# Two-layer decoder on one core: the second tile's residual put before weight splits, and the last queries transposed earlier

## The chip, the cores and the metric

The kernel runs on one core of one Trainium2 chip. The metric is the device time of one execution in microseconds (us), lower is better. The core has TensorE (PE, with PEld for its weight loads), VectorE (DVE), ScalarE (ACT), GpSimd (POOL) and SyncE (SP, which issues the DMAs).

## The reference

A sequence of 256 tokens of width 1024 goes through two layers, each `x <- x + RMSNorm_post(mixer(RMSNorm_pre(x)))`. All arithmetic is float32. Layer 0 is a chunked gated linear attention. Layer 1 is a sparse attention with three branches: compressed blocks, selected blocks and a window. For these sizes the selected and window branches see all keys up to the causal limit. Cut to what matters here:

```
def reference(x, positions, pre_norm, post_norm, ...):
    for i in range(2):
        h = rms_norm(x, pre_norm[i])
        y = gla_mixer(h, ...) if i == 0 else nsa_mixer(h, positions, ...)
        x = x + rms_norm(y, post_norm[i])
    return x

def nsa_mixer(h, positions, w_in, b_gate, ..., w_out):
    q, kc, vc, ks, vs, kw, vw, gl, z = split(h @ w_in)
    q, kc, ks, kw = rope(each, positions)        # q is also scaled by 1/8
    ...
    o = sum over branches of sigmoid(gl + b_gate) * attention(q, branch)
    return (o * silu(z)) @ w_out
```

## The kernel before, in words

**Tiles.** The 256 tokens are two tiles (t = 0, 1) of 128 rows. A float32 product is made from three fp32r matmuls: each operand is split into a rounded part `hi` and a rest `lo`, and hi*hi, hi*lo and lo*hi are summed (`mm3`, lines 211 to 213). Weights come in chunks of up to 512 columns (`Chunk`): a DMA brings two rows of 128 (`raw`, four buffers), ACT writes `hi` (line 190) and DVE or POOL writes `lo` (line 196). Which engine writes `lo` is listed per chunk in `LOS`; for the chunk of the selected keys, `ch_ks`, it is DVE for the rows k = 0 to 3 and POOL for 4 to 7. `hi` and `lo` have eight buffers each.

**The order of the work.** The order on each engine is made when the program is built: a scheduler plays the program through in its own simulated time and takes, on each engine, the earliest traced instruction that is ready in that time. `after(a, b)` forces a to be issued after b. `chain` lines up projections on PE in the order written; instructions outside it, such as most transposes, fall where the scheduler finds room. `paced` is a hint that ties weight splits to the progress of another projection. Buffers of one tag are shared by all tiles of that tag.

**The layer boundary.** For each tile, `out_proj` (line 340) makes layer 0's output in two halves n = 0, 1 in PSUM. `residual` (line 263) follows: ACT squares each half (line 269, with a sum), DVE adds the sums (lines 271, 274), POOL takes the power (line 275), DVE multiplies each half by the norm's row (line 276) and adds the result to X (line 281). Its two tiles `yg` share the tag `xg` (two buffers) with the tile of the same name in `pre_T`. `pre_T` (line 298) transposes X on PE (line 302), scales it (DVE, line 307) and splits it into `hT` (ACT line 310, DVE line 311). `rms` (line 318) squares X for the next norm. After both tiles, `ch_kc` (compressed keys and values) and `ch_ks` (selected keys and values) are split; `ch_ks.split_unit(ks_after)` issues the two `hi` of its first unit after the last line 310 of tile 0, and `ch_ks.split()` does the other three units with no such tie. Then `kc_part(0)`, `ks_part(0)`, `kc_part(1)` and `ks_part(1)` project: each is 24 matmuls of 512 columns into one of two `acc` banks. `kc_part` also ropes its keys (lines 821 to 827) and transposes the result (line 853, 32 small matmuls); for t = 0 it transposes the position vectors (line 846). Loads of the next weights reuse layer 0's memory, the row of its post norm too, which line 276 reads last.

**The attention stage.** `q_steps(p, t)` projects and ropes 8 of the 16 heads for a tile; `q_T(p, t)` transposes them on PE (line 982) into a bank of tag `t` (two banks) and copies them in halves by ACT and DVE (lines 987, 988) into a tile of tag `qS` (six buffers). A `Unit(g, t)` is one of four groups of heads in one tile: `scores` (line 1020, four heads), softmax (DVE 1025, ACT 1027), weighing by POOL (line 1061), `values` with transposes of the weights (line 1091, 1111, banks of tag `t`), copies (1095, 1097), and matmuls (1105, 1129). `finish` gates the result and splits it into `ofT` of its tile; the four tiles of `ofT` have the tag `qS` too. `z_steps(p)` is a projection in 8 steps (k) of 12 chained matmuls. `out_steps(t)` is the last projection; its weights `ch_o` are split under a pace by the steps of `z_steps(1)`. Near the end the program reads, in order: `q_T(1, 0)`, the splits of `ch_z[1]`, `q_steps(1, 1)`, `unit(2, 0)`, `q_T(1, 1)`, `z_steps(1)`, `unit(3, 0)`, `out_steps(0)`, the four units of tile 1, `out_steps(1)`.

Of the kernel before, what the change touches and what calls it, by code (L numbers as in the profile page):

```python
# [10 lines left out]
F32R = mybir.dt.float32r  # L11
I32 = mybir.dt.int32
AF = mybir.ActivationFunctionType
# [3 lines left out]
P = 128  # L17
# [70 lines left out]
def hybrid_kernel(ctx: ExitStack, tc: tile.TileContext, x, positions, pre_norm, post_norm,  # L88
# [9 lines left out]
    def nm(s):  # L98
        _n[0] += 1
        return f"{s}_{_n[0]}"  # L100

    def bank(tag="t"):
        return ps.tile([P, 512], F32, tag=tag, name=nm(tag), bufs=BANKS[tag])
# [4 lines left out]
    def after(ins, prev):  # L108

        if prev is not None:  # L110
            tc.add_manual_dep(ins.ins, prev.ins.name, mybir.DependencyInfo(
                mybir.DependencyClass.NoSync, mybir.DependencyReason.DATA), reason="issue order")
        return ins
# [103 lines left out]
    def chain(first, final):  # L217

        after(first, last[0])
        last[0] = final  # L220
# [34 lines left out]
    def rstd_of(ss, n, m, by=1.0):  # L255
# [4 lines left out]
        nc.gpsimd.tensor_tensor(r[:, :m], v[:, :m], half[:, :m], op=ALU.pow)  # L260
        return r

    def residual(t, o, gb):

        ss = base.tile([P, 8], F32, tag="ss", name=nm("ss"), bufs=4)
        yg = [base.tile([P, H], F32, tag="xg", name=nm("yg"), bufs=2) for _ in range(2)]

        def done(n):
            nc.scalar.activation(yg[n], o[n], AF.Square, accum_out=ss[:, n:n + 1])  # L269
            if n == 0:  # L270
                nc.vector.tensor_scalar(ss[:, 2:3], ss[:, 0:1], D * EPS, None, op0=ALU.add)
            else:

                nc.vector.tensor_add(ss[:, 4:5], ss[:, 1:2], ss[:, 2:3])
                nc.gpsimd.tensor_tensor(ss[:, 3:4], ss[:, 4:5], half[:, :1], op=ALU.pow)
            nc.vector.scalar_tensor_tensor(yg[n], o[n], float(D ** 0.5), gb[:, n * H:(n + 1) * H], op0=ALU.mult,  # L276
                                           op1=ALU.mult)
            if n == 1:
                for m in range(2):
                    xx = X[:, t, m * H:(m + 1) * H]  # L280
                    nc.vector.scalar_tensor_tensor(xx, yg[m], ss[:, 3:4], xx, op0=ALU.mult, op1=ALU.add)
        return done
# [12 lines left out]
        nc.scalar.activation(hi, bv, AF.Copy)  # L295
        nc.vector.tensor_sub(lo, bv, f(hi))

    def pre_T(t, c, layer, hT, tag, prev=None):

        b = bank(tag)  # L300
        for k in range(4):
            m = nc.tensor.transpose(b[:, k * P:(k + 1) * P], X[:, t, (c * 4 + k) * P:(c * 4 + k + 1) * P], ident)
            if layer == t == 0:
                chain(m, m)
        xg = base.tile([P, 4, P], F32, tag="xg", name=nm("xg"), bufs=2)
        g = gT[:, layer * KT + c * 4:layer * KT + c * 4 + 4]
        nc.vector.tensor_tensor(xg, b.rearrange("p (k n) -> p k n", k=4), g.unsqueeze(2).to_broadcast([P, 4, P]),
                                op=ALU.mult)
        hi, lo = (a[:, c * 4:c * 4 + 4, t * P:(t + 1) * P] for a in hT)
        m = after(nc.scalar.activation(hi, xg, AF.Copy), prev)  # L310
        nc.vector.tensor_sub(lo, xg, f(hi))  # L311
        return m

    onesr = base.tile([P, P], F32R, tag="onesr", name="onesr")
    nc.gpsimd.tensor_copy(onesr, ones)
# [458 lines left out]
    for t in range(NT):  # L774
        out_proj(t, ch_o, oT, gpost)
        for c in range(2):
            last_hi = pre_T(t, c, 1, hT, "t")
        if t == 0:
            ks_after = last_hi
        rs1.append(rms(t)[0])  # L780
        for tab in (CSt, SNt):
            nc.vector.tensor_scalar(tab[:, t], tab[:, t], rs1[t], None, op0=ALU.mult)
# [3 lines left out]
    lp = ctx.enter_context(tc.tile_pool(name="l2", bufs=1))  # L786
    ch_kc.split()
    ch_ks = Chunk(w_in, N_KS, 512).load()
    ch_ks.split_unit(ks_after)
    ch_ks.split()  # L790
    vs_sb = lp.tile([P, NT, 256], F32, tag="vs", name="vs_sb")
    vw_sb = lp.tile([P, NT, 256], F32, tag="vw", name="vw_sb")
# [23 lines left out]
    def rope(o, nh, t, twice):  # L816

        ov = o.rearrange("p (h a d) -> p h a d", a=2, d=HD)
        t1 = lp.tile([P, 8, 2, HD], F32, tag="rt1", name=nm("rt1"), bufs=2)
        t2 = lp.tile([P, 8, 2, HD], F32, tag="rt2", name=nm("rt2"))  # L820
        nc.vector.tensor_mul(t1[:, :nh], ov, CSt[:, t].unsqueeze(1).to_broadcast([P, nh, 2, HD]))
        for a in range(2):
            nc.vector.tensor_mul(t2[:, :nh, a, :], ov[:, :, 1 - a, :],
                                 SNt[:, t, a, :].unsqueeze(1).to_broadcast([P, nh, HD]))
        a, b = (y[:, :nh].rearrange("p h a d -> p h (a d)") for y in (t1, t2))
        if not twice:
            nc.gpsimd.tensor_add(a, a, b)
            return a
        r = cp.tile([P, nh, 2, DH], F32, tag="dup", name=nm("dup"), bufs=2)
        nc.gpsimd.tensor_add(r, *(y.unsqueeze(2).to_broadcast([P, nh, 2, DH]) for y in (a, b)))  # L830
        return r
# [5 lines left out]
            nc.tensor.transpose(b[:, g * P:(g + 1) * P], r[:, g].rearrange("p e d -> p (e d)"), ident)  # L837
        return b

    def kc_part(t):  # L840
        o = proj(ch_kc, hT, t)
        rv = cp.tile([P, GROUPS, DH], F32, tag="rv", name=nm("rv"), bufs=2)
        nc.scalar.activation(rv, o[:, 256:512].rearrange("p (g d) -> p g d", d=DH), AF.Copy, scale=rs1[t])
        if t == 0:
            b = bank("o")
            nc.tensor.transpose(b[:, :32], vecs, ident[:32, :32])
            nc.vector.tensor_copy(vT, b[:, :32])

        b = bank()
        for kv, r in enumerate((rope(o[:, :256], 4, t, False), rv)):  # L850
            for g in range(GROUPS):
                for two in range(2):
                    nc.tensor.matmul(b[two * 64:(two + 1) * 64, kv * 256 + g * 64:kv * 256 + (g + 1) * 64], r[:, g],
                                     ident[:, two::2], start=(kv == g == 0), stop=True, skip_group_check=True)
        bv = b.rearrange("p (k g c r) -> p k g c r", k=2, g=GROUPS, r=8)
        for half in range(2):

            c0 = 1 if half and not t else 0
            n = 8 - c0
            at = t * 8 + c0 - half  # L860
            for kv in range(2):
                v = vT[:, kv * 16 + half * 8:kv * 16 + half * 8 + 8]
                nc.vector.tensor_tensor(flat[:, half, kv, :, :, at:at + n].rearrange("p r g c -> p g c r"),
                                        bv[:, kv, :, c0:], v.unsqueeze(1).unsqueeze(1)
                                        .to_broadcast([P, GROUPS, n, 8]), op=ALU.add)
# [6 lines left out]
    def ks_part(t):  # L872
        o = proj(ch_ks, hT, t)
        nc.scalar.activation(vs_sb[:, t, :], o[:, 256:512], AF.Copy, scale=rs1[t])
        k_T(o, t, (1 - t) * P)

    kc_part(0)
    ks_part(0)

    w1 = []  # L880

# [55 lines left out]
    def pe(m):  # L937
        return m
# [13 lines left out]
                done(o)  # L952
            yield 1

    def proj_T_steps(chunk, done):
        o = [bank("acc") for _ in range(2)]
        for k in range(KT):
            for j in range(4):
                a, b = mm3(o[j // 2][:, (j % 2) * S:(j % 2 + 1) * S], chunk.part(k, j * P, (j + 1) * P),
                           [h[:, k, :] for h in hT], k == 0 and j % 2 == 0, k == KT - 1, skip_group_check=True)  # L960
                chunk.mm.setdefault(2 * k, a)
                chunk.mm[2 * k + 1] = a
                chain(a, b)
            if k == KT - 1:
                done(o)
            yield 1

    qS, qr = {}, {}

    def q_steps(p, t):  # L970

# [5 lines left out]
    def q_T(p, t):  # L977

        b = bank()
        r = qr[p, t]  # L980
        for m in range(4):
            pe(nc.tensor.transpose(b[:, m * P:(m + 1) * P], r[:, 2 * m:2 * m + 2].rearrange("p h d -> p (h d)"), ident))
        q = lp.tile([P, 2, 4, P], F32R, tag="qS", name=nm("qS"), bufs=6)
        bv = b.rearrange("p (m n) -> p m n", m=4)
        h = (slice(0, 64), slice(64, 128))
        for a in range(2):
            nc.scalar.activation(q[h[a], a], bv[h[a]], AF.Copy)
            nc.vector.tensor_sub(q[h[1 - a], a], bv[h[a]], f(q[h[a], a]))
        qS[p, t] = q

    def z_steps(p):
        def done(o):
            for j in range(2):
                gate_of(o[j], zT[:, p * 4 + j * 2:p * 4 + j * 2 + 2, :])
        return proj_T_steps(ch_z[p], done)

    def small(n, tag):
        return ap_.tile([P, n], F32, tag=tag, name=nm(tag), bufs=2)
# [199 lines left out]
    q_T(0, 0)  # L1198
    l2a.close()
    ap_ = ctx.enter_context(tc.tile_pool(name="l2b", bufs=1))  # L1200
    ofT = [[lp.tile([P, KT, P], F32R, tag="qS", name=nm("ofT"), bufs=6) for n in "hl"] for t in range(NT)]
    ch_o = [Chunk(nsa_w_out[0], c * 512, 512) for c in range(2)]
    U = {(g, t): Unit(g, t) for g in range(GROUPS) for t in range(NT)}

# [16 lines left out]
    run(q_steps(1, 1))  # L1221
    unit(2, 0)
    q_T(1, 1)
    run(z_steps(1))
    unit(3, 0)
    for g in range(2, 4):
        U[g, 0].finish()
    for k in (0, 2, 4, 6):
        for n in range(2):
            ch_o[n].load(k, k + 2).split((ch_z[1], k + 2 * n + PA[12]))  # L1230
    run(out_steps(0))
    for g in range(GROUPS):
        unit(g, 1)
        U[g, 1].finish()
# [31 lines left out]
```

## Time and profile before

| | before |
|---|---|
| median of 3 runs | 296.37 us (296.13 to 296.43) |
| profiled execution, its own time | 296.34 us |
| its span in the trace | 294.3 us |
| PE busy | 281.9 us, 96% of the span |
| DVE, POOL, ACT busy | 203.9, 178.7, 178.5 us |
| mean granted TensorE clock | 0.993 of 2.4 GHz |

The profiled execution's time is its span plus 2.04 us around it. "Busy" counts the time in which an engine had an instruction in work. Matmuls overlap, so a busy PE can still be a waiting PE; the start of one matmul to the start of the next tells more than the length of either. A row of a timeline gives start, length, engine, line, operation, what is written and read, shapes, and in brackets the engine's idle time before it with what ended that.

### The profile page before, as it was taken

Reading aid. Unit: us, or ns where it says so; the run is one execution under the profiler, and the core shown is the slowest. Engines: PE = TensorE matmul, PEld = TensorE weight load, DVE = VectorE, ACT = ScalarE, POOL = GpSimd, SP = SyncE. Lnnn points to the kernel's source line nnn. Section 1 sums busy time; section 2 is a strip of 40 time slices with the busy share of each in tenths; the row PEclk is TensorE's granted clock in tenths of the full one; section 3 lists DMA queues with packets and bytes.
Section 4 is the critical chain, followed back from the end, with each engine's and each line's share of the span. In section 5 each row is a group of like instructions: output and inputs, shape, how many; then the busy total and the mean of one; then the engine's idle time right before and its main releaser. Section 6 shows DMA issues by size and latency. Waiting matters only on the chain.

```text
span 294.3 us, 5427 instructions
## 1 busy us (share of the span) xinstructions
PE 281.9 (96%) x1836; PEld 238.1 (81%) x1836; DVE 203.9 (69%) x515; ACT 178.5 (61%) x464; POOL 178.7 (61%) x207
## 2 busy tenths in 40 slices
PE   8999999999999999889999999999999899999991
PEld 7888999999999887668898789986889667678560
DVE  1779668854989968577469668797539976585323
ACT  4896788676665665545427436486278797565311
POOL 1496968985376033823539194569799779366400
PEclk9999999999999999999999999999999999999997
DMA  7997589114667255189897475704353000010001
GB/s 213 403 399 208 146 247 292 39 67 145 213 206 224 74 145 143 28 198 358 266 377 220 145 209 155 211 1 155 132 149 136 4 0 2 0 72 2 0 0 71
DMA packets 28300, 44.56 MB, mean 151 GB/s; under 512 B 2865, under 2 KB 12513, under 8 KB 28274
## 3 DMA queue, kind: packets, MB, share of 16 engines
q1 hardware_dynamic: 28242, 44.23, 47.7%
q8 instruction: 14, 0.23, 0.3%
q14 instruction: 12, 0.10, 0.1%
q10 hardware_dynamic: 32, 0.01, 0.0%
HBM read 43.18 MB, written 1.05 MB: 150 GB/s over the span
## 4 chain that ended last, share of the span: by engine, by line
PE 75%; DVE 8%; issue 7%; POOL 4%; ACT 3%; DMA 1%; SPq 0%; DVEq 0%; POOLq 0%; ACTq 0%
PE acc L213 13%; PE acc L212 13%; PE acc L211 13%; PE s L211 4%; PE s L212 4%; PE s L213 4%; PE s L468 4%; PE o L1105 4%; PE s L1020 3%; PE t L1091 3%; PE o L904 2%; DVE lo L196 2%; DMA raw<-in_gla_w_in_dram 1%; PE o L1129 1%; POOL lo L196 1%
## 5 line engine op out<-in xcount | busy, mean ns | idle before, releaser
L196 POOL TENSOR_TENSOR lo<-raw,hi 128x512 fp32r<-128x512 f32 (+2 forms) x63 | 83.6, 1350 | 41.8 <-ACT hi L190 41.8
L190 ACT ACTIVATE hi<-raw 128x512 fp32r<-128x512 f32 (+2 forms) x120 | 62.7, 581 | 17.7 <-DMA raw<-in_nsa_w_in_dram 6.1
L196 DVE TENSOR_TENSOR lo<-raw,hi 128x512 fp32r<-128x512 f32 (+2 forms) x57 | 56.1, 1006 | 11.2 <-ACT hi L190 11.0
L212 PE MATMUL acc<-hT,hi 128*128 128x256 f32 x160 | 45.0, 282 | 0.0
L211 PE MATMUL acc<-hT,hi 128*128 128x256 f32 x160 | 45.0, 281 | 0.0
L213 PE MATMUL acc<-hT,lo 128*128 128x256 f32 x160 | 44.5, 281 | 0.0
L1061 POOL TENSOR_SCALAR P<-P,cf,gates 128x128 f32<-128x128 f32 (+1 forms) x64 | 33.9, 545 | 14.2 <-DVE cf L1057 9.2
L213 PE MATMUL acc<-hi,hT 128*128 128x512 f32 (+2 forms) x104 | 36.0, 346 | 0.8 <-DVE hT L311 0.8
L211 PE MATMUL acc<-hi,hT 128*128 128x512 f32 (+2 forms) x104 | 35.8, 345 | 0.8 <-DVE yg L276 0.7
L212 PE MATMUL acc<-lo,hT 128*128 128x512 f32 (+2 forms) x104 | 35.5, 341 | 0.0
L1027 ACT ACTIVATE P<-P,mn 128x128 f32<-128x128 f32 (+1 forms) x64 | 28.4, 445 | 9.3 <-DVE mn L1025 8.9
L212 PEld LDWEIGHTS acc<-hT,hi 128*128 128x128 f32 x160 | 30.1, 188 | 0.3
L211 PEld LDWEIGHTS acc<-hT,hi 128*128 128x128 f32 x160 | 30.0, 188 | 0.1
L213 PEld LDWEIGHTS acc<-hT,lo 128*128 128x128 f32 x160 | 29.8, 188 | 0.0
L1025 DVE CUSTOM_DVE_ANT_0 P<-s,c 128x128 f32<-128x128 f32 (+1 forms) x64 | 20.8, 350 | 5.7 <-PE s L1020 3.5
L211 PEld LDWEIGHTS acc<-hi,hT 128*128 128x128 f32 x104 | 19.6, 188 | 3.7 <-ACT yg L269 1.2
L213 PEld LDWEIGHTS acc<-hi,hT 128*128 128x128 f32 x104 | 19.6, 188 | 3.3 <-DVE hT L311 1.7
L212 PEld LDWEIGHTS acc<-lo,hT 128*128 128x128 f32 x104 | 19.6, 188 | 1.8
L1091 PE MATMUL t<-c,P 128*128 128x128 f32 x96 | 17.6, 287 | 0.7 <-POOL P L1061 0.3
L440 POOL TENSOR_TENSOR lo<-raw,hi 128x512 fp32r<-128x512 f32 (+1 forms) x9 | 12.3, 1388 | 9.7 <-ACT hi L436 9.6
L1091 PEld LDWEIGHTS t<-c,P 128*128 128x128 f32 x96 | 10.8, 140 | 6.6 <-issue 3.1
L1020 PE MATMUL s<-kTh,qS 128*128 128x272 f32 (+1 forms) x48 | 14.5, 316 | 0.1
(271 smaller groups left out, 668.1 us busy)
## 6 DMA issues: line engine op xcount, KB each, us to landing
raw<-in_nsa_w_in_dram SPq DMA_DIRECT2D x24, 512.0 KB, 4.4
raw<-in_gla_w_in_dram SPq DMA_DIRECT2D x12, 512.0 KB, 5.5
raw<-in_gla_w_out_dram SPq DMA_DIRECT2D x8, 512.0 KB, 4.3
raw<-in_nsa_w_out_dram SPq DMA_DIRECT2D x8, 512.0 KB, 4.2
raw<-in_nsa_w_in_dram SPq DMA_DIRECT2D x8, 280.0 KB, 6.1
raw<-in_gla_w_in_dram SPq DMA_DIRECT2D x6, 344.0 KB, 3.4
home<-in_gla_w_in_dram SPq DMA_DIRECT2D x4, 512.0 KB, 6.7
w<-in_nsa_ck_w_dram SPq DMA_DIRECT2D x4, 512.0 KB, 7.4
```

Source lines behind the costliest of these rows:

```text
L190: m = after(nc.scalar.activation(hi[:, j, :n], raw[:, j, :n], AF.Copy), prev)
L196: eng.tensor_sub(lo[:, j, :n], raw[:, j, :n], f(hi[:, j, :n]))
L211: m = nc.tensor.matmul(o, a[0], b[0], start=start, stop=False, **kw)
L212: nc.tensor.matmul(o, a[0], b[1], start=False, stop=False, **kw)
L213: return m, nc.tensor.matmul(o, a[1], b[0], start=False, stop=stop, **kw)
L440: line(e, eng.tensor_sub(lo[:, j, :n], raw[:, j, :n], f(hi[:, j, :n])))
L468: m = nc.tensor.matmul(o[t][:, :chunk.n], hT[i][:, k, t * P:(t + 1) * P], w[j], start=(k == b == 0), stop=(k == KT - 1 and b == 2))
L1020: pe(nc.tensor.matmul(o, q[i], k[:, g, c0:c1], start=(m == 0), stop=(m == 1)))
L1025: nc.vector.tensor_tensor_reduce(out=o, in0=src, in1=masks[br], op0=ALU.add, op1=ALU.min, scale=-0.125, scalar=3.0e38, accum_out=self.mn[: ...
L1027: nc.scalar.activation(o, o, AF.Exp, scale=-1.0, bias=self.mn[:, j:j + 1], accum_out=self.sm[:, j:j + 1])
L1061: nc.gpsimd.tensor_scalar(o, o, cf[:, i * 2 + br:i * 2 + br + 1], gates[:, t, 4 * g + 2 * h + i, br + 1:br + 2], op0=ALU.mult, op1=ALU.mult)
L1091: pe(nc.tensor.transpose(b[:, i * P:(i + 1) * P], self.Pt[i][:, c0:c0 + P], ident))
```

## The change

At the boundary, the splits of `ch_ks` are tied to the last square of the second tile's residual in place of the last `hi` of the first tile's `hT`. `kc_part(0)` ropes its keys first and then runs `ks_part(0)` in its middle, and the transpose of the position vectors joins the chain on PE. In the attention stage, the matmuls of `z_steps(1)` at k = 1 are issued after the transposes of `q_T(1, 0)`, and those at k = 4 after the ones of `q_T(1, 1)`. The tiles of `ofT` for t = 1 leave the tag `qS`; they become the two halves of one tile under the tag that held `hT`'s hi part.

```
     def residual(t, o, gb):
...
-            nc.scalar.activation(yg[n], o[n], AF.Square, accum_out=ss[:, n:n + 1])
+            squared[0] = nc.scalar.activation(yg[n], o[n], AF.Square, accum_out=ss[:, n:n + 1])
...
         for c in range(2):
-            last_hi = pre_T(t, c, 1, hT, "t")
-        if t == 0:
-            ks_after = last_hi
+            pre_T(t, c, 1, hT, "t")
...
-    ch_ks.split_unit(ks_after)
+    ch_ks.split_unit(squared[0])
     ch_ks.split()
...
-    def kc_part(t):
+    def kc_part(t, then=None):
...
+        rk = rope(o[:, :256], 4, t, False)
         if t == 0:
+            then()
             b = bank("o")
-            nc.tensor.transpose(b[:, :32], vecs, ident[:32, :32])
+            m = nc.tensor.transpose(b[:, :32], vecs, ident[:32, :32])
+            chain(m, m)
...
-        for kv, r in enumerate((rope(o[:, :256], 4, t, False), rv)):
+        for kv, r in enumerate((rk, rv)):
...
-    kc_part(0)
-    ks_part(0)
+    kc_part(0, lambda: ks_part(0))
...
-    def proj_T_steps(chunk, done):
+    def proj_T_steps(chunk, done, behind={}):
...
+                if j == 0:
+                    after(a, behind.get(k))
                 chain(a, b)
...
-            pe(nc.tensor.transpose(b[:, m * P:(m + 1) * P], r[:, 2 * m:2 * m + 2].rearrange("p h d -> p (h d)"), ident))
+            qt[p, t] = nc.tensor.transpose(b[:, m * P:(m + 1) * P], r[:, 2 * m:2 * m + 2].rearrange("p h d -> p (h d)"),
+                                           ident)
...
-    ofT = [[lp.tile([P, KT, P], F32R, tag="qS", name=nm("ofT"), bufs=6) for n in "hl"] for t in range(NT)]
+    ofT = [[lp.tile([P, KT, P], F32R, tag="qS", name=nm("ofT"), bufs=6) for n in "hl"]]
...
-    run(z_steps(1))
+    run(z_steps(1, {1: qt[1, 0], 4: qt[1, 1]}))
...
     run(out_steps(0))
+    both_of = base.tile([P, KT, S], F32R, tag="hTh", name="ofT1")
+    ofT.append([both_of[:, :, :P], both_of[:, :, P:]])
```

## Rows read from the trace of the kernel before

**Rows 1.** Windows: busy us of PE, PEld, DVE, ACT, POOL; then PEclk, DMA

```profile
116.00:122.00 6.00, 5.54 (x23) 4.06 (x22) 4.37 (x10) 5.26 (x12) 3.32 (x3) 1.00 0.04 14
122.00:128.00 6.00, 5.72 (x25) 4.62 (x26) 3.35 (x9) 1.92 (x5) 3.41 (x6) 1.00 0.44 90
128.00:133.00 5.00, 3.66 (x46) 2.69 (x45) 4.52 (x12) 2.15 (x4) 1.72 (x2) 1.00 0.97 269
...
231.00:239.00 8.00, 6.84 (x42) 4.77 (x43) 6.55 (x49) 7.48 (x33) 8.00 (x20) 1.00 0.01 3
239.00:247.00 8.00, 7.64 (x53) 5.69 (x54) 7.37 (x33) 6.81 (x24) 5.71 (x13) 1.00 0.00 0
247.00:285.00 38.00, 37.65 (x228) 25.78 (x225) 19.59 (x78) 18.52 (x60) 18.22 (x35) 1.00 0.04 15
```

**Rows 2.** Timeline of PE at the layer boundary (start, length, engine, line, idle before)

```profile
122.28 0.47 PE L211 MATMUL acc<-hi,hT 128*128 128x512 f32 x1 [0.75 <-DVE yg L276]
...
127.95 0.60 PE L302 MATMUL t<-c,x_sb 128*128 128x128 f32 x4
```

**Rows 3.** Waits of PE over the whole span (us in total, times, longest)

```profile
PE acc L213 <- DVE hT L311: 0.8, 1, 0.8
...
PE t L853 <- DVE vT L847: 0.5, 1, 0.5
```

**Rows 4.** Timeline of ACT at the layer boundary

```profile
115.85 4.26 ACT L190 ACTIVATE hi<-raw 128x512 fp32r<-128x512 f32 x8
120.02 0.57 ACT L269 ACTIVATE yg<-s 128x512 f32<-128x512 f32 x1
```

**Rows 5.** Timeline of DVE at the layer boundary

```profile
109.25 3.48 DVE L196 TENSOR_TENSOR lo<-raw,hi 128x512 fp32r<-128x512 f32 x2
...
115.38 1.29 DVE L311 TENSOR_TENSOR hT<-xg,hT 128x512 fp32r<-128x512 f32 x2
116.59 2.49 DVE L196 TENSOR_TENSOR lo<-raw,hi 128x512 fp32r<-128x512 f32 x4
...
124.54 1.97 DVE L281 SCALAR_TENSOR_TENSOR x_sb<-yg,ss,x_sb 128x512 f32<-128x512 f32 x2 [0.96 <-POOL ss L275]
```

**Rows 6.** Timeline of POOL at the layer boundary

```profile
118.68 5.32 POOL L196 TENSOR_TENSOR lo<-raw,hi 128x512 fp32r<-128x512 f32 x4 [5.05 <-ACT hi L190]
123.93 0.58 POOL L275 TENSOR_TENSOR ss<-ss,cols 128x1 f32<-128x1 f32 x1
```

**Rows 7.** The DMA queue's own waits

```profile
SPq L125 <- DVE yg L276: 9.0, 1, 9.0
```

**Rows 8.** Timeline of PE, 186 to 237 us

```profile
186.25 0.29 PE L1020 MATMUL s<-kTh,qS 128*128 128x272 f32 x1
...
208.66 0.28 PE L211 MATMUL acc<-hT,hi 128*128 128x256 f32 x1
208.78 0.28 PE L212 MATMUL acc<-hT,hi 128*128 128x256 f32 x1
...
213.29 0.30 PE L1111 MATMUL t<-c,cS 128*64 128x128 f32 x1
...
214.33 0.66 PE L982 MATMUL t<-c,rt 128*128 128x128 f32 x4
...
222.84 0.29 PE L1020 MATMUL s<-kTh,qS 128*128 128x272 f32 x1
...
236.75 0.27 PE L1111 MATMUL t<-c,cS 128*64 128x128 f32 x1
236.86 0.60 PE L982 MATMUL t<-c,rt 128*128 128x128 f32 x4
```

**Rows 9.** Timeline of POOL, 192 to 231 us

```profile
192.46 1.75 POOL L1061 TENSOR_SCALAR P<-P,cf,gates 128x128 f32<-128x128 f32 x4 [0.45 <-DVE cs L1074]
...
210.36 1.29 POOL L827 TENSOR_TENSOR rt<-rt,rt 128x512 f32<-128x512 f32 x1 [1.69 <-PE t L1091]
...
230.72 3.47 POOL L1061 TENSOR_SCALAR P<-P,cf,gates 128x128 f32<-128x128 f32 x8 [2.07 <-DVE cS L1072]
```

More of the change, by code (lines that the diff above doesn't have):

```diff
@@ L261, in rstd_of @@
         return r
+    squared = [None]
     def residual(t, o, gb):
@@ L296, in split_bank, with pre_T @@
         nc.vector.tensor_sub(lo, bv, f(hi))
-    def pre_T(t, c, layer, hT, tag, prev=None):
+    def pre_T(t, c, layer, hT, tag):
         b = bank(tag)
@@ L309, in pre_T @@
         hi, lo = (a[:, c * 4:c * 4 + 4, t * P:(t + 1) * P] for a in hT)
-        m = after(nc.scalar.activation(hi, xg, AF.Copy), prev)
+        nc.scalar.activation(hi, xg, AF.Copy)
         nc.vector.tensor_sub(lo, xg, f(hi))
-        return m
     onesr = base.tile([P, P], F32R, tag="onesr", name="onesr")
@@ L966, in proj_T_steps @@
             yield 1
-    qS, qr = {}, {}
+    qS, qr, qt = {}, {}, {}
     def q_steps(p, t):
@@ L989, in q_T, with z_steps @@
         qS[p, t] = q
-    def z_steps(p):
+    def z_steps(p, behind={}):
         def done(o):
@@ L994, in done @@
                 gate_of(o[j], zT[:, p * 4 + j * 2:p * 4 + j * 2 + 2, :])
-        return proj_T_steps(ch_z[p], done)
+        return proj_T_steps(ch_z[p], done, behind)
     def small(n, tag):
```

## The prediction, made before the changed kernel was run

> **What bounds the kernel now.** I read the windows first, because the question is where TensorE (PE) still has time to lose. In 247 to 285 us it is busy for 37.65 of 38 us: nothing is to be had there but work itself [rows 1]. The granted clock is 1.00 in every window read, the upper level of 2.4 GHz, so no stretch is slow for its clock. Two places have holes. At the layer boundary, 116 to 133 us, PE is not busy for 0.46 + 0.28 + 1.34 = 2.08 us; in the attention stage, 231 to 247 us, for 1.16 + 0.36 = 1.52 us [rows 1]. Together 3.6 us: an upper end for what this change can take away, as it removes no work.
>
> The timeline and the waits of PE name the boundary's three holes. The selected keys' projection of tile 0 starts at 122.28 after 0.75 us of waiting for line 276, the residual that still holds the `acc` bank [rows 2]. After its end, at 127.95, come the transposes of tile 1's X [rows 2], then a wait of 0.5 us in which the `t` banks are held, and one of 0.8 us for tile 1's `hT` [rows 3]. All three go back to one thing: tile 1's residual is late. ACT runs eight `hi` of the selected keys' weights from 115.85 for 4.26 us and squares only at 120.02 [rows 4]. The squares need the two `xg` buffers, and those are free when DVE ends line 311, at 115.38 + 1.29 = 116.67 [rows 5]. So the first square starts 3.35 us later than it could. POOL adds to it: its four `lo` last from 118.68 to 124.00, and only then comes the residual's power [rows 6].
>
> **The change at the boundary.** It adds and removes no work here; it swaps the order of eight `hi` and two squares.
>
> *What comes earlier.* The two squares start near 116.7 in place of 120.02 and take 0.57 us each with a sum of about 0.1 us, so both are done by about 118.0. POOL has no `lo` then and takes the power at once (0.58 [rows 6]). X of tile 1 was done at 124.54 + 1.97 = 126.51 [rows 5]; now: 118.0, 0.15 for the sum, 0.58, then 1.97 at most, about 120.8. That is 5.7 us earlier. The bank is free well before 121.5, so the 0.75 goes; tile 1's transposes fall into the running projections, so the 0.5 and the 0.8 can go. Gain at most 2.08.
>
> *What comes later.* The eight `hi` start at about 118.0 in place of 115.85, 2.1 later. The selected keys' projection takes 127.95 - 122.28 = 5.67 us for eight k [rows 2], 0.71 each. Without its wait it starts at 121.53; k = 0 wants its `lo` at about 121.8, k = 4 at 124.6, k = 7 at 126.7. POOL's `lo` of k = 7, which ended at 124.00, ends at about 126.1, or 126.7 if the 0.58 us power of the next norm goes between: just in time. DVE's four `lo` took 2.49 us together, 0.62 each [rows 5]; from 120.8 they are done at 121.4 to 123.3, and wanted from 121.8 to 123.9: again just in time. But two `lo` that DVE ran beside POOL's took 3.48 us, 1.74 each [rows 5]. Were all four so slow, the last would end at 120.8 + 7.0 = 127.8, 3.9 late. So this term lies between a gain of 2.08 and a loss of 3.9 - 2.08 = 1.8. I take a gain of 1.7: near the upper end, as POOL's `lo` begin only when half of DVE's are done, less 0.4 for one operand that comes late.
>
> The Trainium skill ("SBUF — State Buffer", "Who interferes with whom") says that a VectorE instruction with two SBUF inputs and a GpSimd instruction that reads SBUF share a read interface, and that the one that comes second waits out the other. The row agrees in direction (1.74 beside 0.62); by that rule the loss just given is the likely sum wherever both engines split, and it is the third rival below.
>
> *The rest of this part.* Weight loads of the next chunks queue on SP behind line 276, which reads memory that they overwrite: one wait of 9.0 us [rows 7]. It shrinks by as much as line 276 comes earlier, and everything behind it in that queue moves along. No row of PE's waits in that stretch names a DMA, so this gives nothing; its cover, if it went the other way, is the time until those weights are split. The transpose of the position vectors is one small matmul, and line 853's 32 go behind it; what they feed is read much later. I cost both at nothing, hidden in PE's order; bare, they would cost the 0.5 us of [rows 3] again.
>
> **The change in the attention stage.** `q_T(1, 0)` stands at 214.33, and the third group's scores, which need it, only at 222.84 [rows 8]. `q_T(1, 1)` stands at 236.86 although its rope was done at 210.36 + 1.29 = 211.65 [rows 8, 9]. Both times it comes right behind the transpose of line 1111 of the group before it in the program (213.29 and 236.75 [rows 8]). So I read the two `t` banks as handed out in program order, and `q_T(1, 1)` as locked behind the third group's own transposes. The buffers for the queries that the change frees remove the second lock, not this one.
>
> *The gain.* The gate projection starts at 208.66 and spaces its matmuls by 0.12 us [rows 8], 1.4 us for a k. `q_T(1, 0)` then stands before k = 1, at about 211.5; with four half copies the scores start near 213.2, nearly 10 us earlier. POOL's weighing of the third and fourth groups then leaves the window around 230.72 [rows 9], where PE's 1.52 us are lost. Gain at most 1.52.
>
> *The price.* k = 4 now waits for `q_T(1, 1)`, and everything chained behind it too, `out_steps(0)` included; the splits of `ch_o` are paced by these steps and move with them. What PE can do meanwhile: 36 matmuls of k = 1 to 3 (36 x 0.12 = 4.3), the scores of the third and fourth groups and of the first of tile 1 (32 x about 0.12 = 3.8), and some 0.9 of values: from 211.8 to about 220.8. The third group's path, from scores to `q_T(1, 1)`: the first group went from scores at 186.25 to the end of its weighing at 192.46 + 1.75 = 194.21, 8.0 us [rows 8, 9]; with transposes, a copy and the queries' own, 9.5. The third group needed 236.86 - 222.84 = 14.0 [rows 8]. So `q_T(1, 1)` is ready between 213.2 + 9.5 = 222.7 and 227.2, and PE's wait lies between 1.9 and 6.4 us; it is nothing if the banks are not handed out so. Against the 1.52, this part lies between a gain of 1.52 and a loss of 4.9. I take a wait of 1.0, between none and the first group's path, as POOL has few `lo` in that stretch when `ch_o` is held back: a gain of 0.5.
>
> **Sum.** The profiled execution took 296.34 us, 0.03 under the median of the runs shown: 296.34 - 1.7 - 0.5 = 294.1 us.
>
> **The rivals.** *Both places close fully:* 296.34 - 2.08 - 1.52 = 292.7. For it: only order changes; against it: the margins above are tenths.
>
> *Slower: the gate projection waits for `q_T(1, 1)`.* With the third group's path as long as before, PE loses 6.4 us in the middle of `z_steps(1)` and gets 1.52 and 1.7 back: 296.34 + 6.4 - 3.2 = 299.5. It decides once that path passes 9.5 + 2 us or so. For it: the order of the banks [rows 8]; against it: the first group's 8.0 us.
>
> *Slower: DVE splits beside POOL at the boundary.* All four `lo` at 1.74: 296.34 + 1.8 - 0.5 = 297.6. For it: the row at 109.25; against it: the row at 116.59 [rows 5].
>
> *The change doesn't do what it says.* Only the first unit's two `hi` are tied to the square. If the scheduler puts the other six ahead of it, the squares gain two `hi` of 0.53 us, 1.07; the wait of 0.75 goes, the two later ones mostly stay, and a wait in the gate projection eats it: 296.1.
>
> **How the numbers follow.** The forecast has a chance of 0.48, both places closing 0.20, the wait in the gate projection 0.15, DVE beside POOL 0.08, no effect 0.09. About 0.2%, 0.6 us, is what a measurement of this kernel can tell from no change. Faster: 0.48 + 0.20 = 0.68. Same: 0.09. Slower: 0.15 + 0.08 = 0.23. The forecast's own range, from the terms' smaller errors, is 292.9 to 295.7. The range asked for reaches from 291.9, a little under the first rival, up to 298.3: it takes in no effect and DVE beside POOL and leaves out the longer half of the wait in the gate projection.
>
> **What the changed profile would show.** Right: on ACT the squares of tile 1 directly behind line 310 and before the eight `hi`; PE's waits for lines 276 and 311 gone; line 302 of tile 1 before the selected keys' projection ends; line 982 for the last queries within the gate projection, the third group's scores before 215; PE busy for over 15.5 us of the 16 that answer to 231 to 247. Wrong: a wait of PE over 2 us before k = 4 of the gate projection, named after POOL's line 1061 or a copy of line 1095 or 1097; a wait of PE for line 196 in the selected keys' projection; or squares that still stand behind `hi`.

## The result, and the profile after

The kernel after the change takes **304.97 us** (median of 4 runs, 303.32 to 305.77), the kernel before beside it 296.40: a ratio of 1.0282, with an interval of 1.0233 to 1.0332. It is slower by some 8.6 us. The profiled execution is the longest of the four, 305.77 us, with a span of 303.5 and a granted clock of 0.984. In this kernel lines 269 and 271 of before are 271 and 273, 276 is 278, 281 is 283, 982 is 986, 987 is 992, 988 is 993, 1020 is 1025, 1061 is 1066, 1072 is 1077, 1077 is 1082, 1091 is 1096, 1105 is 1110 and 1111 is 1116.

The windows come first, as ahead of the prediction (busy us of PE, PEld, DVE, ACT, POOL; then PEclk, DMA share, GB/s):

```profile
116.00:122.00 6.00, 5.94 (x25) 4.22 (x24) 5.69 (x12) 5.78 (x13) 1.39 (x3) 1.00 0.34 101
...
216.00:224.00 8.00, 6.17 (x35) 4.46 (x35) 6.75 (x54) 6.12 (x29) 4.21 (x10) 1.00 0.38 126
224.00:231.00 7.00, 5.08 (x38) 3.92 (x39) 3.42 (x18) 6.97 (x25) 7.00 (x18) 1.00 0.01 4
231.00:239.00 8.00, 5.68 (x46) 5.21 (x44) 7.97 (x3) 2.73 (x5) 7.22 (x6) 1.00 0.18 66
239.00:247.00 8.00, 6.76 (x20) 5.56 (x21) 7.71 (x17) 5.45 (x14) 2.94 (x2) 0.57 0.24 66
```

At the layer boundary the 2.08 us of [rows 1] are down to 0.06, all in the first window (PE is busy throughout from 122 to 133). In the attention stage PE is now idle for 1.83 + 1.92 + 2.32 + 1.24 = 7.31 us between 216 and 247, where before it was idle for 1.52 [rows 1]; and in the last of these windows the granted clock is 0.57. DVE does three operations from 231 to 239 and is busy for 7.97 us. PE's longest waits, 3.6 us and 1.4 us for line 993 on DVE and 1.0 us for line 1082 on POOL, stand in its timeline below.

None of the boundary's waits in [rows 2, 3] is left. **The boundary** on ACT, DVE and POOL shows why, one line or two of each engine's timeline:

```profile
117.34 0.60 ACT L271 ACTIVATE yg<-s 128x512 f32<-128x512 f32 x1 [0.22 <-DVE hT L313]
...
118.53 4.26 ACT L190 ACTIVATE hi<-raw 128x512 fp32r<-128x512 f32 x8
```

```profile
119.99 1.41 DVE L283 SCALAR_TENSOR_TENSOR x_sb<-yg,ss,x_sb 128x512 f32<-128x512 f32 x2
121.32 1.89 DVE L196 TENSOR_TENSOR lo<-raw,hi 128x512 fp32r<-128x512 f32 x3
```

```profile
118.96 0.55 POOL L277 TENSOR_TENSOR ss<-ss,cols 128x1 f32<-128x1 f32 x1 [4.15 <-DVE ss L276]
...
121.36 6.74 POOL L196 TENSOR_TENSOR lo<-raw,hi 128x512 fp32r<-128x512 f32 x4 [1.56 <-ACT hi L190]
```

The squares stand right behind `hT` and ahead of the eight `hi`, the power comes at once, and X is done at 119.99 + 1.41 = 121.40, where it was 126.51 [rows 5].

**The attention stage**, PE's timeline with its two pauses:

```profile
216.54 0.39 PE L1025 MATMUL s<-kTh,qS 128*128 128x272 f32 x1
...
218.46 0.39 PE L1025 MATMUL s<-kTh,qS 128*128 128x272 f32 x1 [1.41 <-DVE qS L993]
...
228.27 0.30 PE L1116 MATMUL t<-c,cS 128*64 128x128 f32 x1 [1.02 <-POOL cS L1082]
228.41 0.60 PE L986 MATMUL t<-c,rt 128*128 128x128 f32 x4
228.76 0.36 PE L211 MATMUL acc<-hT,hi 128*128 128x256 f32 x1
...
240.24 1.09 PE L1096 MATMUL t<-c,P 128*128 128x128 f32 x4 [3.56 <-DVE qS L993]
240.98 0.78 PE L211 MATMUL acc<-hi,ofT 128*128 128x512 f32 x1
...
245.82 0.47 PE L213 MATMUL acc<-hi,ofT 128*128 128x512 f32 x1
246.13 0.39 PE L211 MATMUL acc<-hi,ofT 128*128 128x512 f32 x1
246.35 0.39 PE L212 MATMUL acc<-lo,ofT 128*128 128x512 f32 x1
```

*The first pause.* The last queries (228.41) still stand right behind the third group's transpose of line 1116 (228.27), and k = 4 of the gate projection, tied to them, comes at 228.76. From the third group's first score to those transposes it takes 228.41 - 216.54 = 11.9 us, and PE has too little else: 3.75 us idle from 216 to 231. The longest piece of it, 1.41 us, waits for the second half of the copy of the queries (1, 0).

*The second pause* of 3.56 us waits for the second half of the last queries' copy. After it the output projection's matmuls come every 4.84 / 11 = 0.44 us (12 from 240.98 to 245.82), then every 0.22: the lower of the clock's two levels, 1.2 GHz, right behind PE's longest wait, costs 11 x 0.22 = 2.4 us. DVE shows what held the copy, and POOL beside it:

```profile
230.45 0.69 DVE L993 TENSOR_TENSOR qS<-t,qS 64x512 fp32r<-64x512 f32 x1 [1.50 <-ACT qS L992]
231.17 8.20 DVE L196 TENSOR_TENSOR lo<-raw,hi 128x512 fp32r<-128x512 f32 x2
239.40 0.69 DVE L993 TENSOR_TENSOR qS<-t,qS 64x512 fp32r<-64x512 f32 x1
```

```profile
230.74 7.48 POOL L196 TENSOR_TENSOR lo<-raw,hi 128x512 fp32r<-128x512 f32 x6
```

Line 196's own row gives the longest single one (minimum, median and maximum in ns):

```profile
L196 DVE TENSOR_TENSOR lo<-raw,hi x57: 423/831/7597, 34.0 to 247.2; 128x512 fp32r<-128x512 f32 x44, 128x280 fp32r<-128x280 f32 x9, 128x344 fp32r<-128x344 f32 x4
```

So of the two DVE `lo` that DVE's order has between the halves of the copy, one lasts 7.6 us (0.62 each elsewhere [rows 5]; before, the longest of all was 1.81). It ends at about 238.8, 0.55 behind a burst of six POOL `lo` (230.74 + 7.48 = 238.22) that run at 1.25 each, as if nothing were beside them.

### The profile page after: what moved, and what is told of

Read it like the earlier page. It is cut to its first block, busy times and chain, and to the rows that moved or that the text cites. A ratio compares the mean times of both kernels' runs of the same rounds, so it can differ in the third digit from the quotient of the medians.

```text
span 303.5 us, 5427 instructions
## 1 busy us (share of the span) xinstructions
PE 285.9 (94%) x1836; PEld 242.0 (80%) x1836; DVE 210.0 (69%) x515; ACT 177.8 (59%) x464; POOL 177.8 (59%) x207
## 4 chain that ended last, share of the span: by engine, by line
PE 77%; DVE 8%; issue 7%; POOL 3%; ACT 2%; DMA 2%; SPq 0%; DVEq 0%; POOLq 0%
PE acc L211 14%; PE acc L213 14%; PE acc L212 14%; PE s L211 4%; PE s L212 4%; PE s L213 4%; DVE lo L196 4%; PE s L469 4%; PE s L1025 3%; PE o L1110 3%; PE o L906 2%; PE t L1096 2%; DVE P L1030 2%; DMA raw<-in_gla_w_in_dram 2%; POOL lo L441 1%
## 5 line engine op out<-in xcount | busy, mean ns | idle before, releaser
L196 DVE TENSOR_TENSOR lo<-raw,hi 128x512 fp32r<-128x512 f32 (+2 forms) x57 | 60.0, 1076 | 11.6 <-ACT hi L190 11.5
L1066 POOL TENSOR_SCALAR P<-P,cf,gates 128x128 f32<-128x128 f32 (+1 forms) x64 | 32.7, 525 | 17.9 <-DVE cf L1062 17.5
L1096 PEld LDWEIGHTS t<-c,P 128*128 128x128 f32 x96 | 11.5, 143 | 7.7 <-issue 5.7
L1025 PE MATMUL s<-kTh,qS 128*128 128x272 f32 (+1 forms) x48 | 15.4, 331 | 2.1 <-DVE qS L993 1.4
```

The lines of the kernel that those rows point to most:

```text
L196: eng.tensor_sub(lo[:, j, :n], raw[:, j, :n], f(hi[:, j, :n]))
L1025: pe(nc.tensor.matmul(o, q[i], k[:, g, c0:c1], start=(m == 0), stop=(m == 1)))
L1066: nc.gpsimd.tensor_scalar(o, o, cf[:, i * 2 + br:i * 2 + br + 1], gates[:, t, 4 * g + 2 * h + i, br + 1:br + 2], op0=ALU.mult, op1=ALU.mult)
L1096: pe(nc.tensor.transpose(b[:, i * P:(i + 1) * P], self.Pt[i][:, c0:c0 + P], ident))
```

## Experiments

Each was run beside the kernel before on the same chip; ratios are to that. "After" below is the kernel after the change.

**1 and 2: each half alone.** The boundary without the attention stage's part (`run(z_steps(1))`, and the queries' buffers as before), and the attention stage's part on the kernel before.

```
-    run(z_steps(1, {1: qt[1, 0], 4: qt[1, 1]}))
+    run(z_steps(1))
...
-    ofT = [[lp.tile(..., tag="qS", ...) for n in "hl"]]
+    ofT = [[lp.tile(..., tag="qS", ...) for n in "hl"] for t in range(NT)]
...
```

> The boundary part alone: the attention stage is the one of before, with no order forced on z_steps(1) and ofT in the old buffers. Theory (the whole loss is in the attention stage, and the boundary part does what the prediction said): PE has no wait over 0.3 us between 116 and 133 us and the kernel takes 294.4 us (293.9 to 295.0), 2 us under before. Rival (the boundary change moves other work so that the attention stage suffers even without the forced order): 297 us or more.

> The attention part alone: the boundary is the one of before. Theory: the whole loss is here, so it takes 305 to 308 us, before plus about 9 to 11, with a wait of PE over 3 us behind a copy of line 988 and a granted clock near half in the windows right after. Rival (the two parts only harm each other together): 297 us or less.

The boundary alone takes 294.14 us, a ratio of 0.9907 (0.9888 to 0.9926); the attention part alone 307.3 us, 1.0354 (1.0320 to 1.0388). The boundary's windows in the first, then PE's longest wait in the second:

```profile
115.00:121.00 6.00, 5.94 (x25) 4.21 (x24) 5.69 (x11) 5.78 (x13) 1.30 (x3) 1.00 0.34 105
121.00:127.00 6.00, 6.00 (x32) 4.96 (x31) 5.11 (x10) 3.75 (x9) 6.00 (x4) 1.00 0.63 148
```

```profile
PE t L1094 <- DVE qS L991: 3.6, 1, 3.6
```

All of the loss, and more, is the attention stage's, and it doesn't need the boundary's new order.

**3: no tie, the freed buffers stay.** `run(z_steps(1))` in the kernel after.

> The changed kernel with no order forced on z_steps(1); the buffers of ofT stay as changed. Theory (the forced order behind the last queries' transposes is what costs, not the buffers): 293.5 to 295.5 us, as the boundary part alone; line 986 for the last queries stays behind the third group's line 1116. Rival (the freed buffers themselves reorder the stage for the worse): 298 us or more. A second thing to read: if the last queries' transposes come early here, then the buffers were the lock and not the order of the t banks.

294.28 us, 0.9911 (0.9887 to 0.9936). The queries' transposes, although a buffer is free for them, come where they came before, behind line 1116:

```profile
235.05 0.27 PE L1116 MATMUL t<-c,cS 128*64 128x128 f32 x1
235.16 0.60 PE L986 MATMUL t<-c,rt 128*128 128x128 f32 x4
```

**4: the queries first.** The last queries' transposes are traced ahead of the third group, both ties stay.

```
+    q_T(1, 1)
     unit(2, 0)
-    q_T(1, 1)
```

> The changed kernel with q_T(1, 1) traced ahead of unit(2, 0), so that its bank of tag t comes before the third group's in program order; the forced order at k = 1 and k = 4 stays. Theory (k = 4 waited for the third group's whole path because the t banks are handed out in program order): the transposes of the last queries stand right behind those of q_T(1, 0), the wait before k = 4 is gone, and the time is 293 to 296 us. Rival (the wait comes from the forced order itself, wherever the bank stands): 300 us or more.

293.79 us, 0.9889 (0.9863 to 0.9916). They come at 213.45 now, and the tie at k = 4 costs nothing:

```profile
213.45 0.66 PE L986 MATMUL t<-c,rt 128*128 128x128 f32 x4
```

Run 3 shows that a free buffer alone doesn't bring the last queries forward, run 4 that an earlier place in the program does. That the place acts through the `t` banks fits run 3, where the gate projection, which the program has later, goes ahead of them; a run with the queries first and the old buffers was not made.

**5: no POOL burst.** All `lo` of the output weights go to DVE, both ties stay.

```
-LOS = (..., (0, 1, 2, 3, 4, 5, 6, 7), (1, 2, 5))
+LOS = (..., (), ())
```

> The kernel after the change, with both forced places kept; only the `lo` of the two chunks of output weights all go to VectorE, so that GpSimd has no burst of line 196 around 231 us. Theory (two losses: the pause ahead of k = 4, and behind it VectorE's second half of line 993, held by one `lo` of 7.6 us beside GpSimd's burst of six): the pause ahead of k = 4 stays, from about 218 to 228; no VectorE `lo` takes over 1.5 us, TensorE's wait for line 993 falls from 3.6 us to under 1.5, the clock of that stretch stays near 1.00 or falls less, and the time is about 301 us (299 to 302.5). Rival (the second loss belongs to the forced order itself, the burst only stands beside it): the wait of 3 us or more and the low clock stay, 304 us or more. Second rival (VectorE, with ten more `lo`, becomes the bound): waits for line 196 appear in the output projection, over 304 us.

297.76 us (296.93 to 298.91), 1.0029 (1.0010 to 1.0048): 7.2 us less than after, and 3 us less than the theory's number (its range began at 299). The wait behind line 993's second half is gone, no DVE `lo` is long, and the first pause stays as it was (1.84 + 1.91 = 3.75 us idle), with the clock partly low behind it (0.76 in the second window):

```profile
216.00:224.00 8.00, 6.16 (x32) 4.14 (x31) 7.04 (x57) 6.63 (x33) 3.93 (x9) 1.00 0.18 63
224.00:231.00 7.00, 5.09 (x28) 4.28 (x29) 4.76 (x16) 6.98 (x22) 7.00 (x15) 0.76 0.01 4
231.00:239.00 8.00, 8.00 (x63) 7.01 (x61) 7.66 (x15) 5.90 (x11) 1.11 (x2) 1.00 0.42 130
239.00:247.00 8.00, 8.00 (x46) 6.38 (x45) 5.58 (x22) 3.45 (x14) 1.30 (x4) 1.00 0.00 0
```

Against the boundary alone, run 5 loses 297.76 - 294.14 = 3.6 us. Its pause of 3.75 us and its low clock (7 x 0.24 = 1.7) come to 5.4; PE is without any idle time from 231 to 247 here, where [rows 1] have 1.52, which leaves 3.9 against the 3.6 measured. What run 5 takes away, the second pause with its low clock, is the 7.2 us. The two were measured in different sittings; by the ratios it is 7.5.

**6: bursts by themselves.** A kernel with nothing but subtractions, n on one engine and m on the other.

> Measures by itself how long a subtraction of one of VectorE and GpSimd takes beside a burst of subtractions of the other; nothing of the reference is computed. One engine issues n subtractions (128x512, both inputs in SBUF) one behind the other, the other engine m of its own, which may start behind the first of these; n and m are 1/1, 2/1, 3/1, 6/1 and 6/3, first with GpSimd's burst, then with VectorE's. Theory (the one that comes second is held until the other's burst is over): with GpSimd's burst VectorE's subtraction lasts about 0.6 us alone and grows by about 1.2 us for each further one of GpSimd, to 6 us or more at n = 6; the other way it grows by about 0.6 each, to 4 us or so. Rival (they take turns, instruction by instruction): VectorE's subtraction lasts at most about 1.9 us at any n, and GpSimd's at most about 1.9 us.

The theory fell: the engines take turns. Beside a POOL burst of six, three DVE operations last 1.7 us each, and POOL's own grow from 1.26 to 1.59 on average (DVE's timeline, of the first two, then POOL's):

```profile
24.08 3.40 DVE L115 TENSOR_TENSOR other<-x_sb,head 128x512 f32<-128x512 f32 x2 [6.03 <-POOL head L110]
```

```profile
24.01 7.93 POOL L112 TENSOR_TENSOR burst<-x_sb,res 128x512 f32<-128x512 f32 x5
```

**7 and 8: the first tie alone, and no tie with the queries first.** `{1: qt[1, 0]}` in the kernel after; and the edit of run 4 with `run(z_steps(1))`.

> The kernel after the change without the second forced place: k = 1 of the gate projection still stands behind the queries (1, 0), k = 4 behind nothing. Theory (the loss is the tie of k = 4 to the last queries alone): 294.3 us (293.7 to 295.0), the same as without any forced order, no wait of TensorE over 1 us between 205 and 250 us. Rival (the queries (1, 0) ahead of k = 1 bring the third group's scores forward and set off the trouble by themselves): 297 us or more, with waits for line 993 or line 1066 in that stretch.

> The boundary's new order, the freed buffers, and the last queries' transposes traced ahead of the third group, with no forced order in the gate projection. Theory (each tie costs or gives nothing once the transposes are early; what is left is the boundary's gain): 293.8 us (293.3 to 294.4), the same as with both ties and the early transposes (293.79). Rival (the ties give something of their own, by bringing the third group's weighing forward): 295 us, over 0.2% more than that kernel.

Run 8 came out as expected, 293.87 us, 0.9907 (0.9882 to 0.9932). Run 7 didn't: 297.37 us (295.48 to 298.13), 1.0008 (0.9984 to 1.0031), so the first tie alone gives the boundary's gain away; the time is the rival's, but the waits that the rival named are not there. Its profiled execution is one of its shortest (295.51) and shows only PE's wait of 1.7 us for POOL's line 1082. POOL weighs the third and fourth groups in one go of twelve there, behind six `lo`, where run 3 has eight behind five; run 7 first, then run 3:

```profile
218.94 9.02 POOL L196 TENSOR_TENSOR lo<-raw,hi 128x512 fp32r<-128x512 f32 x6
227.94 6.21 POOL L1066 TENSOR_SCALAR P<-P,cf,gates 128x128 f32<-128x128 f32 x12
```

```profile
219.72 7.22 POOL L196 TENSOR_TENSOR lo<-raw,hi 128x512 fp32r<-128x512 f32 x5
229.02 3.47 POOL L1066 TENSOR_SCALAR P<-P,cf,gates 128x128 f32<-128x128 f32 x8 [2.07 <-DVE cS L1077]
```

What the longer executions of run 7 lose beyond this, no profile here shows; the granted clock of its ten executions runs from 0.982 to 0.995, lowest in two of the long ones. In run 8 PE is idle for 0.74 and 0.78 us from 224 to 239:

```profile
224.00:231.00 7.00, 6.26 (x32) 5.18 (x32) 6.65 (x37) 5.08 (x21) 3.83 (x6) 1.00 0.02 5
231.00:239.00 8.00, 7.22 (x49) 5.34 (x50) 6.34 (x44) 7.61 (x33) 8.00 (x20) 1.00 0.00 0
```

These 1.52 us are what [rows 1] have from 231 to 247: the attention stage's hole only moved.

**9: the point of entry.** The second burst kernel sweeps where in a POOL `lo` DVE comes in, with `hi` from ACT as in the kernel.

> Measures by itself when a VectorE `lo` is held through a whole burst of GpSimd `lo` and when the two take turns; nothing of the reference is computed. In nine blocks GpSimd runs three fillers and then four `lo` whose `hi` ScalarE made before, VectorE a subtraction from PSUM 32 to 512 wide and then two `lo`, so that its first `lo` comes at another point of GpSimd's first one in each block; in four blocks the `hi` come from a long-done tile; in twelve more GpSimd's single `lo` meets four of VectorE, again at a swept point. Theory (the point at which the second engine comes in decides): at some of the points VectorE's first `lo` lasts over 4 us, at the others at most 1.8, and GpSimd's `lo` lasts over 2.9 us where it comes within 0.1 us of VectorE's start and under 1.8 elsewhere. Rival (it takes something else of the kernel, which is not in these blocks): all blocks take turns, no VectorE `lo` over 1.8 us.

For POOL's bursts the theory fell again: in the thirteen blocks with four POOL `lo`, DVE's 26 come in 0.2 to 1.3 us behind the start of the POOL instruction that each of them meets. The longest DVE `lo` of all 25 blocks is 1.75 us, one of these 26, and no POOL `lo` is over 1.73:

```profile
L131 DVE TENSOR_TENSOR vlo<-x_sb,hi x26: 977/1360/1751, 9.0 to 115.3; 128x512 fp32r<-128x512 f32 x26
```

The other twelve blocks don't do what they were made for: in eleven of them POOL's single `lo` meets one DVE `lo` instead of four, each time 0.47 us behind its own start, and in the first none. So a POOL `lo` that comes in at a swept point of a DVE burst was not measured.

**10: the tie at k = 7** (`{1: qt[1, 0], 7: qt[1, 1]}`).

> The kernel after the change with the last queries tied ahead of k = 7 of the gate projection in place of k = 4; k = 1 stays tied to the queries (1, 0). Theory (the third group's scores are set in behind the steps that are not tied, so the path of about 12 us starts later by as much as the tie does, and TensorE again has too little beside it): the third group's first score stands at about 219 to 221 in place of 216.5, a pause of 3 us or more stays ahead of k = 7; the output weights' splits are no longer held back, so no VectorE `lo` over 2 us and no fall of the clock of the kind seen: 297 to 300 us. Rival (only the place of the tie counts, the path starts when it did): the four microseconds of k = 4 to 6 cover the pause, 294 to 295.5 us.

298.21 us, 1.0038 (1.0023 to 1.0054). The third group's first score moves to 218.92, and the queries still come behind line 1116, after a pause whose longest piece is 1.77 us:

```profile
218.92 0.29 PE L1025 MATMUL s<-kTh,qS 128*128 128x272 f32 x1
...
228.58 1.12 PE L1110 MATMUL o<-pT,vs_sb 128*64 128x256 f32 x4 [1.77 <-ACT pT L1100]
...
230.70 1.06 PE L986 MATMUL t<-c,rt 128*128 128x128 f32 x4
```

The path went with the tie and took 11.8 us again (to the queries' transposes at 230.70), so the rival fell. From 231 to 247 PE has no idle time here either. Two details of the theory fell as well: the pauses are 2.4 us together, not 3, and the clock does fall behind them (0.82 from 224 to 231; line 1110's four matmuls take 1.12 us, not 0.65).

**11: copies first.** The queries (1, 0) are transposed and copied ahead of the first two groups' last step.

```
+    q_T(1, 0)
     for g in range(2):
         U[g, 0].finish()
-    q_T(1, 0)
```

> The kernel after the change with the queries (1, 0) transposed and copied ahead of the first two groups' last step (line 357 and on), so that their copies on ScalarE and VectorE don't stand behind lines 357 and 358; both ties stay. Theory (TensorE's own order, steps 1 to 3 of the gate projection first, sets the start of the third group's scores, the copies only some tenths): the first score moves from 216.5 by under 1.5 us, a pause ahead of k = 4 of over 2 us stays, 303 to 304.5 us if the hold of VectorE stays, 297 to 300 if it goes. Rival (the copies' place is what made the path start late, against the 213.2 of the prediction): the first score at 213 to 214.5, the pause under 1 us, and the time 2.5 us or more under what either case of the theory gives.

305.05 us, 1.0273 (1.0252 to 1.0293), half a microsecond over the theory's 303 to 304.5. The first half of the copy is done at 212.26 + 0.68 = 212.94 now, but the first score moves by 0.9 us only, to 215.62. It still stands behind nearly all of k = 1 to 3, so the copies' place is not what made the path start late (DVE, then PE):

```profile
212.26 0.68 DVE L993 TENSOR_TENSOR qS<-t,qS 64x512 fp32r<-64x512 f32 x1 [2.50 <-ACT qS L992]
```

```profile
215.62 0.28 PE L1025 MATMUL s<-kTh,qS 128*128 128x272 f32 x1
```

The copies' place did make half of the first pause: the 1.41 us of waiting for line 993 are gone, and 1.07 + 0.78 = 1.85 us idle are left from 216 to 231, less than the theory said, with the clock at 0.76 from 224 to 231. The gain is lost at the second pause, which shows best what a held `lo` is. DVE's timeline, then POOL's:

```profile
229.35 10.31 DVE L196 TENSOR_TENSOR lo<-raw,hi 128x512 fp32r<-128x512 f32 x1
```

```profile
229.16 9.95 POOL L196 TENSOR_TENSOR lo<-raw,hi 128x512 fp32r<-128x512 f32 x8
```

One subtraction takes 10.31 us and ends at 239.66, 0.55 behind the last of eight POOL `lo`; PE waits 5.4 us for line 993 behind it.

**12: the copy ahead of the `lo`.** On DVE alone the second half of the queries' copy goes ahead of the output weights' `lo` from the second pair on.

```
...
-                eng.tensor_sub(lo[:, j, :n], raw[:, j, :n], f(hi[:, j, :n]))
+                after(eng.tensor_sub(lo[:, j, :n], raw[:, j, :n], f(hi[:, j, :n])), copied[0] if eng is nc.vector else None)
...
```

> The kernel after the change with one edit of VectorE's order: the last queries' second half copy (line 993) goes ahead of the output weights' `lo` from the second pair on, so that it no longer stands behind the `lo` that lasted 7.6 us. GpSimd's burst and both ties stay. Theory (that copy, held behind the `lo`, made TensorE's wait of 3.6 us and with it the fall of the clock): the copy is done by about 234 in place of 240, the wait for line 993 goes or stays under 1 us, the stretch of half clock goes or shrinks, the pause ahead of k = 4 stays at about 3 us; 297 to 299.5 us, with the held `lo` still there or not. Rival (the output weights are what is late, and TensorE waits for them next): a wait of 2 us or more for line 196 in the output projection, the low clock stays, 302 us or more.

301.66 us (301.05 to 303.47), 1.0193 (1.0152 to 1.0233): 3.3 us less than after (2.6 by the ratios, whose intervals just touch), between theory and rival. The wait for line 993's second half and the low clock are gone (1.00 from 231 to 255), the `lo` is held again (4.9 us of the row's 5.51), and what now stands behind it, the gates' copy out of the `acc` banks on line 363, makes PE wait 2.2 us. DVE, then PE's waits:

```profile
232.51 0.69 DVE L993 TENSOR_TENSOR qS<-t,qS 64x512 fp32r<-64x512 f32 x1 [2.01 <-ACT qS L992]
233.24 5.51 DVE L196 TENSOR_TENSOR lo<-raw,hi 128x512 fp32r<-128x512 f32 x2
```

```profile
PE acc L211 <- DVE zT L363: 2.2, 1, 2.2
```

## Why the prediction was wrong, point by point

**What bounds the kernel** was read rightly: the boundary's three holes went back to tile 1's residual, and with it early all three close.

**The boundary's term** was right, its size a little low: 1.7 us against 2.8 (run 1, 297.1 x 0.0093; by its interval 2.2 to 3.3). The two profiled executions differ by 294.3 - 292.2 = 2.1 us, which is what the three holes come to, my "at most 2.08"; where the other 0.7 of the median come from, no run shows. X was done at 121.40, 0.6 later than worked out, in an execution whose squares came 0.9 later than run 1's (117.34 against 116.44). Of the two `lo` prices I weighed, DVE's three take 1.89 us, 0.63 each, and POOL pays instead: its four take 6.74, not 5.32 [rows 6], and end 128.10, later than the 126.7 that I called just in time, without a wait of PE. The rival of DVE's splits beside POOL at this place fell: where the two engines meet here, it is POOL that waits. Its first `lo` starts 0.04 us behind the first of these three and lasts 2.99 us, until 1.14 behind the last (the maximum of line 196's row):

```profile
L196 POOL TENSOR_TENSOR lo<-raw,hi x63: 790/1293/2988, 38.7 to 245.4; 128x512 fp32r<-128x512 f32 x48, 128x344 fp32r<-128x344 f32 x8, 128x280 fp32r<-128x280 f32 x7
```

The DMA queue's wait of 9.0 us [rows 7] shrinks to 5.1, as written, for nothing.

**That the buffers were not the lock**, but the order in the program, was right (runs 3 and 4); that it is the banks fits both.

**The step that failed** is the price of the tie, "I take a wait of 1.0". The number lies under my own bounds of 1.9 to 6.4, drawn down by the case of no wait, which my own reading of the banks spoke against. But the bounds were wrong too; they had three terms.
- *The path's start.* I had the third group's scores at 213.2, four half copies after the queries' transposes. They came at 216.54, and run 11 shows that the copies were not the reason: PE's own order has all matmuls of k = 1 to 3 ahead of the scores.
- *The cover.* For the same reason the 4.3 us of k = 1 to 3, which I counted as work that PE can do meanwhile, were done before the path began. Run 10 shows the same from the other side: with the tie three k further on, the path starts later too.
- *The path's length*, 11.9 us, lay between my 9.5 and 14.0. With the start at 216.5 and only the scores and values left as cover (3.8 + 0.9), the same sum gives a wait of 4.8 to 9.3 us, and the rival "the gate projection waits", which I priced at 6.4 us and gave 0.15, would have been the forecast. The pause is 3.75 us idle: PE counts as busy for 8.1 of the path's 11.9 us, more than those 4.7.

**The term that was missing** is larger. I wrote that the splits of `ch_o` are paced by these steps and move with them, and put no price on it. Held back until 230, POOL's `lo` come in one burst of six just when DVE has its own between the halves of the last queries' copy. DVE's first is held for the whole burst, PE waits 3.56 us behind it, and the clock falls to its lower level, for another 2.4. Taking the burst away takes 7.2 us off (run 5), taking the copy out from behind it some 3 (run 12).

**The sum:** against the boundary alone the change loses 304.97 - 294.14 = 10.8 us, and 303.5 - 292.2 = 11.3 in the profiled executions. Of these, 0.9 lie ahead of the boundary. PE's idle time between 216 and 247 is 7.31, 5.8 more than run 1's 1.52; the low clock makes 2.4; and behind 255 PE is idle for 7.7 us, where run 1 has 6.6. Some 1.0 us are not assigned.

**The attention stage's gain** of 0.5 to 1.5 us is not there even without a pause: runs 4 and 8 (293.79 and 293.87) can't be told from the boundary alone, and the hole is as large as before in another place (run 8). Where a pause comes first, the hole does close (runs 5 and 10 have no idle time from 231 to 247), and the pause costs more than the 1.52.

The Trainium skill ("SBUF — State Buffer", "Who interferes with whom") says that of a VectorE instruction with two SBUF inputs and a GpSimd one that reads SBUF the later blocks for the whole of the earlier. The 1.75 us of run 9 agree; the 7.6 us in the kernel after and the 10.31 of run 11 last until the end of six and eight instructions and don't.

The best kernels here are the boundary alone, or with the queries first (runs 1, 4 and 8), all near 294 us.

## What to carry to other kernels

Before an in-order engine is tied to a result, look up what stands on that engine between now and the tie: work that the order has already put ahead of the result's path is no cover for it. A pause also moves everything paced by the paused steps; ask in which company that work comes back, and what of a shared order stands behind it. To free a buffer did nothing here while the place in the program still kept the queries back (run 3).

## What the runs showed of the hardware that was not expected

A DVE subtraction with two SBUF inputs was held until the end of a burst of POOL subtractions: through six in the kernel after (7.6 us) and eight in run 11 (10.31 us), each time ending some 0.55 us behind the last, and through what was left of a burst in run 12 (4.9 us). At the boundary one POOL `lo` was held through three of DVE (2.99 us). It is not how the two engines behave in general: in the burst kernels (runs 6 and 9) and in [rows 5] (1.74 us each) they take turns, and in run 9 whatever the point at which DVE came in.

What makes the difference stays open. The held DVE cases have a POOL burst that follows POOL's weighing (lines 1066 and 1082) without a gap, which none of the burst kernels had. That alone is not enough: in the kernel after, a burst of three right behind line 1066 takes turns with DVE's `lo` (POOL, then DVE):

```profile
196.56 3.18 POOL L1066 TENSOR_SCALAR P<-P,cf,gates 128x128 f32<-128x128 f32 x4
199.71 4.23 POOL L196 TENSOR_TENSOR lo<-raw,hi 128x512 fp32r<-128x512 f32 x3
```

```profile
201.15 1.64 DVE L196 TENSOR_TENSOR lo<-raw,hi 128x512 fp32r<-128x512 f32 x1
```

The granted clock isn't the same behind like pauses either: 3.75 us idle from 216 to 231 left it at 1.00 in the kernel after and at 0.76 in run 5.
